# One pinned order for the second chunk's up-projection weights, ahead of the first chunk's convolution

## The chip, the cores and the metric

The kernel runs on one core of a Trainium2 chip. A core has several engines, each with a queue of its own that it works through in order: TensorE (PE, matrix products), VectorE (DVE), ScalarE (ACT), GpSimd (POOL) and SyncE (SP), which here issues nearly all of the DMA transfers. An instruction that depends on another engine waits for a semaphore at the head of its queue, and all that stands behind it waits too. The metric is the time of one execution in device microseconds (us).

## The reference

One layer of a hybrid decoder on 1,024 tokens of width 1,024, after 16 prepended meta tokens. All is in float32.

```python
h = layer_norm(concat(meta, x))
z = h @ w_in + b_in                       # q, k, v, conv input, merge gates
a = sliding_window_attention(q, k, v)     # 8 heads, window 128
c = silu(layer_norm(causal_dwconv(c_val * sigmoid(c_gate), 31 taps)))
mixed = sigmoid(g_attn) * (a @ w_attn_proj) + sigmoid(g_conv) * (c @ w_conv_proj)
h = layer_norm(ALPHA * h + mixed @ w_out)
up = causal_dwconv(h @ ffn_w_up, ffn_dw, ffn_dw_b)      # 3 taps
u, g = split(up, 2)                                     # 2 x 2816 columns
f = (gelu(g) * u) @ ffn_w_down
out = layer_norm(ALPHA * h + f)
```

The change lies in the up projection, `h @ ffn_w_up` with its 3-tap convolution, the gelu and the product `gelu(g) * u`.

## The kernel before

The stages follow each other on TensorE: input projection with the attention and the 31-tap convolution beside it (to about 414 us of the profile), the two branch projections (to 504), the output projection (to 604), the up projection (604 to 1042), the down projection (to 1246) and the last normalization.

**The up projection** makes 22 chunks. Chunk `c` takes 128 gate columns and 128 value columns of `ffn_w_up` (tiles `FC + c` and `c`, 1,024 x 128 each). The product is made by a Strassen-Winograd scheme: the weights' four quadrants `a11`, `a12`, `a21`, `a22` and the activations' four quadrants are first combined into sums, and seven products (`prod`, L1587) take the place of eight. For float32 accuracy each operand is split in a high part (a cast to fp32r on ScalarE) and a low part (raw minus high, on VectorE), and a product is three matrix products high x high, low x high, high x low. The tokens are halved once more in two pieces, `sub` 0 and 1. One of the seven products is 24 matmuls of 256 or 260 columns.

The seven products of a chunk come in the order B11, B21, BT2, BT4, BT1, BT3, B22. They go to four accumulators in PSUM: X (`px`) takes B11, BT2 and BT3 one on top of the other, Z (`pz`) takes B21, V4 (`pw`) BT4, and Y (`py`) BT1 and B22. Between BT2 and BT3 and the like, ScalarE copies what X or Y holds so far (`copy`, L1609). VectorE then puts the four results together (`tt`, L1605): `c11` from Z, later `c22`, `c21` and `c12`.

**Weights.** The generator `up_weights` (L1429) makes a chunk's seven weight operands from two raw tiles `wr` of 512 KB that SyncE loads (`w_rows`, two buffers: the load for the chunk after next waits for the last reader of the tile that it overwrites). In order: `a11` for B11; `a12` for B21; the split of `a22` (for BT4); then three sums on VectorE (L1433): a22 = a21 + a22, a21 = a11 - a21, a11 = a22 - a11; then the split of the new `a11` (BT2), of `a22` (BT1), of `a21` (BT3); a fourth sum, a22 = a12 - a11, and its split (B22). Each split is one cast (`wsplit`, L1414, ScalarE) and one subtraction (L1415, VectorE), 128 x 512 each. The operands lie in a ring of ten places in `RHO` and in tiles `w`; `ring_next` counts them over all chunks, so chunk 0 has 1 to 7 and chunk 1 has 8 to 14. `w_ahead(9)` in `prod` keeps nine operands ahead in the program.

**Convolution.** For each of the four results `conv_ffn` (L1519) takes three small ScalarE steps (L1522 twice, L1524) and two VectorE steps (L1525, L1526); two results go through gelu (L1530), and `f_out` (L1533) multiplies and stores to `fd`, one store a half.

Chunk 0 is made in two passes, `sub` 1 first, because the activations of `sub` 0 come last out of the stage before; the splits of their sums (`split_of`, `bsplit`, L1285) run on VectorE and ScalarE during the first pass. Chunk 1 follows directly. `sums_load` and `sums_form` (L1546, L1552; L1557 to L1560) prepare weights of the down projection: two loads, four sums, two stores a chunk.

**What sets the order.** A list scheduler places the instructions of each engine by its own estimate of when each is ready and by a rank (smaller first; `RK_SUMS` is 470, `RK_CHAIN` for the `tt` and `copy` steps 400, `RK_TURN` 450). `after(x, y)` says only that x stands behind y in the order. `line` strings an instruction behind the one before on a list `lined`; `high` is a like list of ScalarE casts. While `pinned_w` is set, that is for chunk 0's weights, low parts and sums are strung on `lined`. For the first three operands of chunk 1 (`ring_next` to 10) before, a cast was put behind the last of the activation casts and a low part behind a named activation split (`formed`); the rest of chunk 1 was left to the scheduler.

Of the kernel before, what the change touches and what calls it, by code (L numbers as in the profile page):

```python
# [26 lines left out]
OP = mybir.AluOpType  # L27
# [17 lines left out]
FC = DFF // P  # L45
# [14 lines left out]
HW = 514  # L60
# [53 lines left out]
def tile_hybrid_layer(  # L114
# [1291 lines left out]
    def wsplit(src):  # L1406
        i = ring_next[0]
        ring_next[0] += 1
        i %= len(RING)
        if RING[i] is None:  # L1410
            RING[i:i + 2] = wsp_flat()
        t = RING[i]
        hi, lo = t[:, 0:512], t[:, 512:1024]
        cast = nc.scalar.copy(hi, src)  # L1414
        ins = nc.vector.tensor_tensor(lo, src, f32(hi), OP.subtract)  # L1415
        if pinned_w[0]:
            line(ins)
        elif ring_next[0] <= 10:
            after(cast, high[-1])
            after(ins, formed[ring_next[0] - 8])  # L1420
        return hi, lo
# [7 lines left out]
    def up_weights():  # L1429


        def tt(*x):
            ins = nc.vector.tensor_tensor(*x)  # L1433
            if pinned_w[0]:
                line(ins)
# [19 lines left out]

    pinned_w, formed = [True], []
    w_stream = up_weights()
# [60 lines left out]

    def conv_ffn(cc, o):  # L1519
        t = ftmp()  # L1520
# [3 lines left out]
        nc.scalar.activation(t, cc[:, 2:HW], AF.Identity, bias=ffw(3, o), scale=ffw(2, o))  # L1524
        nc.vector.scalar_tensor_tensor(t, cc[:, 1:HW - 1], ffw(1, o), t, OP.mult, OP.add)  # L1525
        nc.vector.scalar_tensor_tensor(t, cc[:, 0:HW - 2], ffw(0, o), t, OP.mult, OP.add)  # L1526
# [49 lines left out]
    for c in range(FC):  # L1576
        Y, V4, Z, X = (pup.tile([P, 1024], F, name=n, tag=n) for n in ("py", "pw", "pz", "px"))
        passes = ((1,), (0,)) if c == 0 else ((0, 1),)
        for subs in passes:
# [7 lines left out]
            def prod(q, bank, first):  # L1587
                if last:
                    w_ahead(9)
                    ah, al = w_ready.pop(0)  # L1590
# [24 lines left out]
            if last and c == 0:  # L1615
                after(high[-2], copied[-1])
            prod(B21, Z, True)
# [5 lines left out]
            if not last:  # L1623
# [5 lines left out]
                form_t3(0, LATE)  # L1629
                for q in (BT2, BT4, BT1, BT3, B22):  # L1630
                    split_of(0, q)
                    formed.append(lined[-1])
                t2_low = formed[0]
                formed[:2] = []
            if last:
                g0 = gelu(conv_ffn(c11, FC + c))
            prod(BT4, V4, True)
# [270 lines left out]
```

## Time and profile before

| what | us |
|---|---|
| median of three runs | 1258.44 (1258.18 to 1258.76) |
| the profiled execution's own time | 1261.86 |
| its span, first to last instruction | 1260.1 |
| 414 to 504 us, branch projections: PE busy | 90.00 of 90.00 |
| 504 to 604 us, output projection: PE busy | 100.00 of 100.00 |
| 1042 to 1246 us, down projection: PE busy | 204.00 of 204.00 |
| 1246 to 1260 us, last normalization: PE busy | 6.00 of 14.00 |

The profile is one execution, recorded by the hardware. In its rows a time is the start from the span's beginning, then the busy time, engine, line, operation, tiles written and read, shape and count; in brackets stands how long the engine was idle before and what ended that. A matmul row of count 12 is one half of one of the seven products.

### The profile page before, as it was taken

Reading aid. Unit: us, or ns where it says so; the run is one execution under the profiler, and the core shown is the slowest. Engines: PE = TensorE matmul, PEld = TensorE weight load, DVE = VectorE, ACT = ScalarE, POOL = GpSimd, SP = SyncE. Lnnn points to the kernel's source line nnn. Section 1 sums busy time; section 2 is a strip of 40 time slices with the busy share of each in tenths; the row PEclk is TensorE's granted clock in tenths of the full one; section 3 lists DMA queues with packets and bytes.
Section 4 is the critical chain, followed back from the end, with each engine's and each line's share of the span. In section 5 each row is a group of like instructions: output and inputs, shape, how many; then the busy total and the mean of one; then the engine's idle time right before and its main releaser. Section 6 shows DMA issues by size and latency. Waiting matters only on the chain.

```text
span 1260.1 us, 23202 instructions
## 1 busy us (share of the span) xinstructions
PE 1242.3 (99%) x9176; PEld 1176.2 (93%) x9176; DVE 1080.4 (86%) x1866; ACT 627.5 (50%) x1280; POOL 7.4 (1%) x8
## 2 busy tenths in 40 slices
PE   8999999999999999999989999999999999999997
PEld 7999999999999999788989999999999998888886
DVE  7988999999978677448989999999899987896697
ACT  7533355655474233344656565665565654445330
POOL 0000000001000000000000000000000000000000
PEclk9999999999999999999999999999999999999999
DMA  6383633332256554222145455553454557999712
GB/s 252 110 300 104 188 98 97 106 97 81 72 159 179 167 155 118 84 100 79 56 151 213 156 207 185 186 209 114 173 210 167 209 204 254 391 354 334 274 61 84
DMA packets 98688, 212.20 MB, mean 168 GB/s; under 512 B 11396, under 2 KB 38596, under 8 KB 98323
## 3 DMA queue, kind: packets, MB, share of 16 engines
q1 hardware_dynamic: 84414, 199.57, 46.5%
q10 hardware_dynamic: 14164, 11.15, 2.8%
q8 instruction: 72, 1.18, 0.4%
q14 instruction: 38, 0.30, 0.1%
HBM read 150.29 MB, written 62.70 MB: 169 GB/s over the span
## 4 chain that ended last, share of the span: by engine, by line
PE 88%; DVE 7%; DMA 3%; ACT 1%; issue 1%; SPq 0%; DVEq 0%; ACTq 0%
PE px L1599 11%; PE ps_x L1754 9%; PE ps_z L340 8%; PE ps_z L343 8%; PE ps_z L344 8%; PE py L1599 8%; PE ps_z L1754 7%; PE ps_p L1172 7%; PE pw L1599 4%; PE pz L1599 4%; PE ps_w L340 2%; PE ps_w L343 2%; PE ps_w L344 2%; PE ps_z L575 2%; PE ps_t L943 1%
## 5 line engine op out<-in xcount | busy, mean ns | idle before, releaser
L340 PE MATMUL ps_z<-RHO,w 128*128 128x256 f32 (+2 forms) x864 | 243.2, 281 | 0.0
L343 PE MATMUL ps_z<-RHO,w 128*128 128x256 f32 (+2 forms) x864 | 242.3, 280 | 0.0
L344 PE MATMUL ps_z<-RHC,w 128*128 128x256 f32 (+2 forms) x864 | 242.2, 280 | 0.0
L343 PEld LDWEIGHTS ps_z<-RHO,w 128*128 128x128 f32 x864 | 162.5, 188 | 0.5
L344 PEld LDWEIGHTS ps_z<-RHC,w 128*128 128x128 f32 x864 | 162.6, 188 | 0.2
L340 PEld LDWEIGHTS ps_z<-RHO,w 128*128 128x128 f32 x864 | 162.5, 188 | 0.1
L749 DVE SCALAR_TENSOR_TENSOR FA<-cin,cdw,FA 128x1026 f32<-128x1026 f32 x120 | 154.3, 1295 | 0.7
L300 ACT CAST w<-wr 128x1024 fp32r<-128x1024 f32 x37 | 38.8, 1048 | 62.6 <-PE ps_z L344 44.5
L1415 DVE TENSOR_TENSOR RHO<-wr,RHO 128x512 fp32r<-128x512 f32 x94 | 64.0, 684 | 2.1 <-ACT RHO L1414 1.7
L1414 ACT CAST RHO<-wr 128x512 fp32r<-128x512 f32 x94 | 57.0, 618 | 17.4 <-DVE wr L1433 10.8
L1433 DVE TENSOR_TENSOR wr<-wr 128x512 f32<-128x512 f32 x88 | 60.1, 683 | 0.2
L758 ACT ACTIVATE FA<-ps_z,colr 128x258 f32<-128x258 f32 (+1 forms) x64 | 30.1, 472 | 59.8 <-PE ps_z L344 46.9
L303 DVE TENSOR_TENSOR w<-wr,w 128x1024 fp32r<-128x1024 f32 x37 | 45.1, 1218 | 7.6 <-ACT w L300 7.4
L1611 ACT COPY FA<-px 128x516 f32<-128x516 f32 (+2 forms) x23 | 13.1, 570 | 72.0 <-PE px L1599 72.0
L1599 PE MATMUL px<-OA,RHO 128*128 128x260 f32 x324 | 44.1, 285 | 4.2 <-ACT RHO L1414 2.4
L1172 PE MATMUL ps_p<-OC,w 128*128 128x256 f32 (+1 forms) x384 | 48.1, 278 | 0.0
L1172 PE MATMUL ps_p<-OA,w 128*128 128x256 f32 (+1 forms) x384 | 47.8, 278 | 0.0
L1172 PEld LDWEIGHTS ps_p<-OC,w 128*128 128x128 f32 x384 | 46.1, 188 | 0.1
L1172 PEld LDWEIGHTS ps_p<-OA,w 128*128 128x128 f32 x384 | 45.9, 188 | 0.0
L1599 PEld LDWEIGHTS px<-OA,RHO 128*128 128x128 f32 x324 | 40.9, 190 | 5.0 <-ACT RHO L1414 2.6
L1415 DVE TENSOR_TENSOR w<-wr,w 128x512 fp32r<-128x512 f32 x60 | 40.8, 685 | 5.2 <-ACT w L1414 5.0
L1414 ACT CAST w<-wr 128x512 fp32r<-128x512 f32 x60 | 36.3, 617 | 13.6 <-DMA wr<-in_w_up_dram 7.4
(457 smaller groups left out, 3117.7 us busy)
## 6 DMA issues: line engine op xcount, KB each, us to landing
wr<-in_w_up_dram SPq DMA_DIRECT2D x44, 512.0 KB, 4.3
wr<-in_w_z_dram SPq DMA_DIRECT2D x29, 512.0 KB, 4.1
OB<-in_w_down_dram SPq DMA_DIRECT2D x24, 512.0 KB, 5.4
fd<-FA SPq DMA_DIRECT2D x44, 256.0 KB, 2.0
FA<-sd SPq DMA_DIRECT2D x15, 512.0 KB, 8.7
qt<-qd SPq DMA_DIRECT2D x28, 256.0 KB, 4.3
OB<-td SPq DMA_DIRECT2D x14, 512.0 KB, 8.7
sgd<-FA ACTq DMA_DIRECT2D x48, 128.0 KB, 2.6
```

What stands on the lines that cost most here:

```text
L300: ins = nc.scalar.copy(hi, raw)
L303: return nc.vector.tensor_tensor(lo, raw, f32(hi), OP.subtract)
L340: ins = nc.tensor.matmul(ps, al, bh, start=i == 0, stop=False)
L343: nc.tensor.matmul(ps, ah, bh, start=False, stop=False)
L344: last = nc.tensor.matmul(ps, ah, bl, start=False, stop=i == n - 1)
L749: nc.vector.scalar_tensor_tensor(acc[c], cin[:, j:j + U], wc, acc[c], OP.mult, OP.add)
L1172: nc.tensor.matmul(ps[:, :b - a], x, rhs(k, hl, a, b), start=k + j == 0, stop=k == 3 and j == 2)
L1414: cast = nc.scalar.copy(hi, src)
L1415: ins = nc.vector.tensor_tensor(lo, src, f32(hi), OP.subtract)
L1433: ins = nc.vector.tensor_tensor(*x)
L1599: ins = nc.tensor.matmul(o, (ah, ah, al)[j][:, k * P:(k + 1) * P], bmat(sub, q, j, k), start=first and i == 0, stop=i == 11, skip_group_ch ...
L1754: nc.tensor.matmul(banks[i], l[:, ts], r[:, ws], start=first and a and x + k == 0, stop=z and x == len(ops) - 1 and k == 2, skip_group_che ...
```

## The change

In words: (1) For operands 8 to 13 of the ring, which are chunk 1's without the last, the casts on ScalarE are strung on `high` in the order in which they are generated, and the low parts on VectorE on `lined`. (2) The three sums of chunk 1 (`ring_next` at 10) are strung on `lined` too; so VectorE has activation splits, low parts of the first three operands, the three sums, the low part of the new `a11`, and then the next low parts in one fixed order. (3) The operands that are generated ahead of products B11 and B21 of chunk 0 get rank `RK_SUMS`. (4) In chunk 0 the first VectorE step of each of the four convolutions (L1525) stands behind the last of `lined` at that point, which is the low part for BT2 of chunk 1. (5) Chunk 1's copy of B11 on ScalarE stands behind the cast for BT2 (`high[7]`), and in chunk 0 the copy after B11 now stands ahead of the fourth activation cast and not ahead of the third. The list `formed` is gone. No instruction is added or removed, none changes its size; the line numbers of the new kernel behind L1417 are up to five higher (L1611 is L1614, L1607 is L1610, L1526 is L1528, L1534 is L1536, L1557 to L1560 are L1559 to L1562).

```diff
-        if pinned_w[0]:
+        if not pinned_w[0] and ring_next[0] <= 13:
+            after(cast, high[-1])
+            high.append(cast)
+        if pinned_w[0] or ring_next[0] <= 13:
             line(ins)
-        elif ring_next[0] <= 10:
-            after(cast, high[-1])
-            after(ins, formed[ring_next[0] - 8])
         return hi, lo
@@ up_weights
         def tt(*x):
             ins = nc.vector.tensor_tensor(*x)
-            if pinned_w[0]:
+            if pinned_w[0] or ring_next[0] <= 10:
                 line(ins)
...
-    def conv_ffn(cc, o):
+    def conv_ffn(cc, o, behind=None):
...
-        nc.vector.scalar_tensor_tensor(t, cc[:, 1:HW - 1], ffw(1, o), t, OP.mult, OP.add)
+        ins = nc.vector.scalar_tensor_tensor(t, cc[:, 1:HW - 1], ffw(1, o), t, OP.mult, OP.add)
+        if behind:
+            after(ins, behind)
         nc.vector.scalar_tensor_tensor(t, cc[:, 0:HW - 2], ffw(0, o), t, OP.mult, OP.add)
@@ prod
                 if last:
-                    w_ahead(9)
+                    with rank(RK_SUMS if c == 0 and q in (B11, B21) else tc.cur_priority):
+                        w_ahead(9)
...
             copy(u13[:, a:b], at(X))
             if last and c == 0:
-                after(high[-2], copied[-1])
+                after(high[3], copied[-1])
+            if c == 1:
+                after(copied[-1], high[7])
...
-                for q in (BT2, BT4, BT1, BT3, B22):
+                split_of(0, BT2)
+                t2_low = lined[-1]
+                for q in (BT4, BT1, BT3, B22):
                     split_of(0, q)
-                    formed.append(lined[-1])
-                t2_low = formed[0]
-                formed[:2] = []
             if last:
-                g0 = gelu(conv_ffn(c11, FC + c))
+                behind = None if c else lined[-1]
+                g0 = gelu(conv_ffn(c11, FC + c, behind))
...
-                f1 = conv_ffn(c22, c)
-                f_out(c, 0, g0, conv_ffn(c21, c))
-                f_out(c, 1, gelu(conv_ffn(c12, FC + c)), f1)
+                f1 = conv_ffn(c22, c, behind)
+                f_out(c, 0, g0, conv_ffn(c21, c, behind))
+                f_out(c, 1, gelu(conv_ffn(c12, FC + c, behind)), f1)
```

How it moves the instructions is seen at three places. The first is VectorE's order around chunk 1's weights. `wr_7241` and `wr_7242` are chunk 1's two raw tiles (`a11`, `a12` and `a21`, `a22`); `pz_7461` is chunk 1's accumulator Z; `FA` and `OB` hold results and convolutions. Before, from the second of the three sums on:

```order
L1433 TENSOR_TENSOR wr_7242<-wr_7241,wr_7242 128x512
L1525 SCALAR_TENSOR_TENSOR FA_78<-OB_81,coll_130,FA_78 128x512
L1525 SCALAR_TENSOR_TENSOR FA_78<-FA_78,coll_130 128x512
L1433 TENSOR_TENSOR wr_7241<-wr_7242,wr_7241 128x512
L1415 TENSOR_TENSOR RHO_80<-wr_7242,RHO_80 128x512
L1526 SCALAR_TENSOR_TENSOR FA_78<-OB_81,coll_130,FA_78 128x512
L1526 SCALAR_TENSOR_TENSOR FA_78<-FA_78,coll_130 128x512
L1525 SCALAR_TENSOR_TENSOR FA_78<-OB_81,coll_130,FA_78 128x512
L1607 TENSOR_TENSOR FA_78<-pz_7461,OB_81 128x516
L1433 TENSOR_TENSOR wr_7242<-wr_7241 128x512
L1415 TENSOR_TENSOR RHO_80<-wr_7242,RHO_80 128x512
L1415 TENSOR_TENSOR RHO_80<-wr_7241,RHO_80 128x512
```

And the change, from the first of the three sums on:

```order
L1433 TENSOR_TENSOR wr_7242<-wr_7242 128x512
L1433 TENSOR_TENSOR wr_7242<-wr_7241,wr_7242 128x512
L1433 TENSOR_TENSOR wr_7241<-wr_7242,wr_7241 128x512
L1415 TENSOR_TENSOR RHO_80<-wr_7241,RHO_80 128x512
L1525 SCALAR_TENSOR_TENSOR FA_78<-FA_78,coll_130 128x512
L1525 SCALAR_TENSOR_TENSOR FA_78<-OB_81,coll_130,FA_78 128x512
L1525 SCALAR_TENSOR_TENSOR FA_78<-FA_78,coll_130 128x512
L1525 SCALAR_TENSOR_TENSOR FA_78<-OB_81,coll_130,FA_78 128x512
L1415 TENSOR_TENSOR RHO_80<-wr_7242,RHO_80 128x512
L1528 SCALAR_TENSOR_TENSOR FA_78<-FA_78,coll_130 128x512
L1415 TENSOR_TENSOR RHO_80<-wr_7242,RHO_80 128x512
L1528 SCALAR_TENSOR_TENSOR FA_78<-OB_81,coll_130,FA_78 128x512
```

The low part of the new `a11` (it reads `wr_7241`) moves from behind three convolution steps, Z's step, the fourth sum and another low part to directly behind its own sum; the convolution of chunk 0 moves behind it. After these rows the change has two more convolution steps, the fourth sum of chunk 1 (it frees tile `wr_7241`), Z's step with `pz_7461`, the two products of `f_out`, and chunk 1's last low part.

The second place is VectorE's order around chunk 2's weights, from raw tiles `wr_7405` (`a11`, `a12`) and `wr_7406` (`a21`, `a22`). Before, from its third low part on, the first two standing just ahead:

```order
L1415 TENSOR_TENSOR w_7238<-wr_7406,w_7238 128x512
L1433 TENSOR_TENSOR wr_7406<-wr_7406 128x512
L1433 TENSOR_TENSOR wr_7406<-wr_7405,wr_7406 128x512
L1415 TENSOR_TENSOR RHO_80<-wr_7406,RHO_80 128x512
L1433 TENSOR_TENSOR wr_7405<-wr_7406,wr_7405 128x512
L1415 TENSOR_TENSOR RHO_80<-wr_7406,RHO_80 128x512
L1433 TENSOR_TENSOR wr_7406<-wr_7405 128x512
L1415 TENSOR_TENSOR w_7238<-wr_7405,w_7238 128x512
L1415 TENSOR_TENSOR RHO_80<-wr_7406,RHO_80 128x512
L1607 TENSOR_TENSOR OB_81<-OB_81 128x516
L1607 TENSOR_TENSOR FA_78<-OB_81,pw_7460 128x516
L1557 TENSOR_TENSOR OB_81<-OB_81 128x512
```

And the change, where `pz_7697` is chunk 2's accumulator Z:

```order
L1610 TENSOR_TENSOR FA_78<-pz_7697,OB_81 128x516
L1528 SCALAR_TENSOR_TENSOR FA_78<-OB_81,coll_130,FA_78 128x512
L1562 TENSOR_TENSOR OB_81<-OB_81 128x512
L1433 TENSOR_TENSOR wr_7406<-wr_7405,wr_7406 128x512
L1415 TENSOR_TENSOR RHO_80<-wr_7406,RHO_80 128x512
L1525 SCALAR_TENSOR_TENSOR FA_78<-FA_78,coll_130 128x512
L1536 TENSOR_TENSOR FA_78<-FA_78 128x512
L1433 TENSOR_TENSOR wr_7405<-wr_7406,wr_7405 128x512
L1415 TENSOR_TENSOR RHO_80<-wr_7406,RHO_80 128x512
L1528 SCALAR_TENSOR_TENSOR FA_78<-FA_78,coll_130 128x512
L1433 TENSOR_TENSOR wr_7406<-wr_7405 128x512
L1415 TENSOR_TENSOR w_7238<-wr_7405,w_7238 128x512
```

Before, all of chunk 2's sums and low parts stood in one piece ahead of chunk 1's results, and the step that reads `pz_7697` came twelve rows after the last row shown. Now they are spread among chunk 1's results and convolutions. Between the first two low parts (which stand behind chunk 1's last) and the rows shown there are, in order: four steps on chunk 1's results and on the down-projection sums (three L1610 and one L1559), three convolution steps, L1560, the third low part, two convolution steps, L1561, the first sum of chunk 2 and one product of `f_out`. The second and third sum of chunk 2 and the low part for its BT2, the last row, stand behind the step that reads chunk 2's own Z.

The third place is ScalarE's order around chunk 3's casts (raw tiles `wr_7611`, `wr_7612`) and the copies of chunk 2's accumulators `px_7698` and `py_7695`. Before:

```order
L1611 COPY FA_78<-px_7698 128x516
L1522 ACTIVATE FA_78<-FA_78 128x1 x2
L1524 ACTIVATE FA_78<-FA_78,coll_130 128x512
L1414 CAST w_7169<-wr_7612 128x512
L1530 ACTIVATE FA_78<-FA_78 128x512
L1414 CAST w_7238<-wr_7612 128x512
L1611 COPY OB_81<-py_7695 128x516
```

And the change:

```order
L1414 CAST RHO_80<-wr_7611 128x512 x2
L1414 CAST RHO_80<-wr_7612 128x512
L1614 COPY FA_78<-px_7698 128x516
L1414 CAST w_7169<-wr_7612 128x512
L1414 CAST w_7238<-wr_7612 128x512
L1414 CAST w_7169<-wr_7611 128x512
L1414 CAST w_7238<-wr_7612 128x512
L1614 COPY OB_81<-py_7695 128x516
```

All seven casts of chunk 3 now stand ahead of the copy of `py_7695`, on top of which chunk 2's B22 is accumulated; before, only five of them did.

On ScalarE the cast for BT2 of chunk 1 stands, in the change, directly behind the last L1524 of chunk 0 and ahead of the copy of chunk 1's X; the table load for gelu and the first gelus stand behind chunk 1's second copy of X. In SyncE's queue the loads `wr_7405`, `fd` store, `wr_7406`, `fd` store, two `OB` loads become `wr_7405`, two `fd` stores, `OB` load, `wr_7406`, `OB` load; and the two loads of chunk 3's raw tiles, which before stood next, now stand behind two stores to `td`, two to `fd` and the two loads of `sums`.

More of the change, by code (lines that the diff above doesn't have):

```diff
@@ L1454, in up_weights @@
             yield p3
-    pinned_w, formed = [True], []
+    pinned_w = [True]
     w_stream = up_weights()
```

## The prediction

> **What bounds the kernel now.** I read the page first, then the stages, then TensorE's waits.
>
> ```profile
> span 1260.1 us, 23202 instructions
> PE 88%; DVE 7%; DMA 3%; ACT 1%; issue 1%; SPq 0%; DVEq 0%; ACTq 0%
> 604.00:651.00 47.00, 42.98 (x344) 41.82 (x343) 42.53 (x77) 28.76 (x59) 0.00 (x0) 0.96 0.28 95
> 651.00:1042.00 391.00, 390.53 (x3363) 390.06 (x3362) 359.25 (x569) 234.26 (x499) 0.00 (x0) 1.00 0.51 187
> ```
>
> The second line is the chain of waits; the last two are stretches: length, then busy time of PE, its weight loads, DVE, ACT and POOL, then the granted clock. PE sets the end. From 651 on it lacks 0.5 us of 391, so nothing is to be won there; from 604 to 651, in chunks 0 and 1, it lacks 4.0 of 47, at a mean clock of 0.96. DVE is 92% busy in the later chunks (359.25 of 391), so what is put off there is caught up slowly. PE's waits from 600 to 700, and PE in order of time:
>
> ```profile
> PE px L1599 <- ACT RHO L1414: 2.4, 1, 2.4
> PE px L1599 <- DVE RHO L1415: 1.4, 1, 1.4
> 625.45 1.59 PE L1599 MATMUL px<-RHC,w 128*128 128x260 f32 x12
> 628.23 1.59 PE L1599 MATMUL pz<-RHO 128*128 128x260 f32 x12
> 629.66 1.52 PE L1599 MATMUL pz<-OC,RHO 128*128 128x256 f32 x12
> 633.58 0.76 PE L1599 MATMUL px<-OA,RHO 128*128 128x260 f32 x4 [2.40 <-ACT RHO L1414]
> 635.70 1.78 PE L1599 MATMUL px<-OA,RHO 128*128 128x260 f32 x8 [1.36 <-DVE RHO L1415]
> 637.28 2.58 PE L1599 MATMUL px<-OC,RHO 128*128 128x256 f32 x12
> 639.70 1.59 PE L1599 MATMUL pw<-OA,RHO 128*128 128x260 f32 x12
> 648.48 1.70 PE L1599 MATMUL py<-RX,RHO 128*128 128x260 f32 x12 [0.26 <-ACT OB L1611]
> 656.98 1.70 PE L1599 MATMUL px<-OA,w 128*128 128x260 f32 x12
> ```
>
> Chunk 1 begins at 625.45, and one product lasts 2.78 (625.45 to 628.23; half of it 1.43). Its third, BT2, waits 2.40 us for the cast of the new `a11`, does four matmuls, and waits 1.36 for the low part. Then matmuls run slow: twelve take 2.42 (637.28 to 639.70). The clock tells why:
>
> ```profile
> 632.68:636.10 3.42, 1.16 (x7) 0.94 (x8) 3.42 (x6) 2.54 (x6) 0.00 (x0) 1.00 0.00 0
> 636.10:639.51 3.41, 3.41 (x18) 3.41 (x18) 3.34 (x6) 0.63 (x1) 0.00 (x0) 0.50 0.81 228
> ```
>
> In a stretch of 3.4 us in which PE was busy for 1.16, the clock stayed; for the next 3.41 it was 0.50, which costs half of that, 1.7. The last PE row is chunk 2's BT2. Nine products at 2.785 behind 625.45 it would begin at 650.5; it begins at 656.98. So all that goes wrong in chunk 1 has cost 6.5 us by then: 2.40 + 1.36 + 0.26 + 1.7, and 0.8 of small steps.
>
> Why is the cast late? ScalarE and VectorE in order of time:
>
> ```profile
> 626.22 0.48 ACT L1522 ACTIVATE OB<-OB 128x1 f32<-128x1 f32 x2 [1.62 <-DVE OB L1607]
> 627.31 0.47 ACT L1522 ACTIVATE FA<-FA 128x1 f32<-128x1 f32 x2
> 630.58 1.28 ACT L1530 ACT_TABLE_LOAD   x1
> 632.41 1.12 ACT L1414 CAST RHO<-wr 128x512 fp32r<-128x512 f32 x2
> 625.10 0.74 DVE L1525 SCALAR_TENSOR_TENSOR FA<-FA,coll 128x512 f32<-128x512 f32 x1
> 625.77 0.42 DVE L1607 TENSOR_TENSOR OB<-OB 128x260 f32<-128x260 f32 x1
> 626.10 0.41 DVE L1607 TENSOR_TENSOR FA<-OB,pw 128x260 f32<-128x260 f32 x1
> 628.64 0.74 DVE L1525 SCALAR_TENSOR_TENSOR FA<-OB,coll,FA 128x512 f32<-128x512 f32 x1
> 629.30 0.74 DVE L1525 SCALAR_TENSOR_TENSOR FA<-FA,coll 128x512 f32<-128x512 f32 x1
> 629.97 0.68 DVE L1433 TENSOR_TENSOR wr<-wr 128x512 f32<-128x512 f32 x1
> 630.57 0.68 DVE L1415 TENSOR_TENSOR RHO<-wr,RHO 128x512 fp32r<-128x512 f32 x1
> 634.36 1.28 DVE L1415 TENSOR_TENSOR RHO<-wr,RHO 128x512 fp32r<-128x512 f32 x2
> 644.61 1.42 DVE L1433 TENSOR_TENSOR wr<-wr 128x512 f32<-128x512 f32 x2
> ```
>
> The third sum (629.97) stands behind convolution steps; the cast then stands behind the table load and a gelu, and the low part, second of the two at 634.36, behind more convolution.
>
> **The change part by part.** No instruction is added, so everything is order. From start to start, a VectorE subtraction of 512 takes 0.60 (629.97 to 630.57), a convolution step 0.66 (628.64 to 629.30), a 260-wide result 0.33 (625.77 to 626.10), a sum that needs the one before 0.71 (half of 1.42); ScalarE's three steps of one convolution take 1.09 (626.22 to 627.31), a cast 0.6.
>
> *Chunk 1, gain.* VectorE is free at 625.10. Three results (1.0) and three sums (2.1): 628.2. ScalarE starts the last three convolutions once the first result stands, at 625.5, and is through at 625.5 + 3 x 1.09 = 628.8; cast to 629.4, low part to 630.1. PE comes to BT2 at 629.66 + 1.36 = 631.0. Both stalls and the half clock go, with 0.9 us to spare. The later operands are in time too: VectorE's rows, four L1525 (2.65), low part for BT1 at 633.3 (PE is there at 636.6), for BT3 at 634.6 (639.4), fourth sum at 637.2, B22's low part at 639.6 (642.1). Chunk 2 could begin at 644.95 in place of 651.4.
>
> *Chunk 2, loss.* Its first raw tile comes free with the fourth sum, at 637.2, which is 1.6 later than before:
>
> ```profile
> 635.67 5.49 DMA wr<-in_w_up_dram
> 641.84 1.29 DVE L1415 TENSOR_TENSOR w<-wr,w 128x512 fp32r<-128x512 f32 x2 [2.40 <-ACT w L1414]
> 649.10 0.58 ACT L1611 COPY OB<-px 128x516 f32<-128x516 f32 x1
> wr<-in_w_up_dram SPq DMA_DIRECT2D x10, 512.0 KB, 3.5
> OB<-in_w_down_dram SPq DMA_DIRECT2D x4, 512.0 KB, 5.1
> sums<-in_w_down_dram SPq DMA_DIRECT2D x2, 512.0 KB, 5.1
> ```
>
> The load took 5.49 there (rows of the chain, of DVE, of a copy on ACT, and of the transfers from 600 to 700 with their median); the median of ten is 3.5. At 5.49 it lands at 642.7 and, as 641.84 follows on 641.16, the low parts start at 643.4 and end at 644.6: in time for B11 and B21. But now VectorE's queue has chunk 1's results and convolutions first. From 644.6: four subtractions (2.4) 647.0; three convolution steps (2.0) 649.0; L1560 and the third low part 650.2; two steps 651.5; L1561, the first sum and a product 653.3; then L1610, which reads chunk 2's own Z (complete at 650.5, so no wait) 653.9; a step 654.6; L1562, second sum, low part 656.4; a step and a product 657.7; third sum 658.3. The cast for BT2 follows at 659.0; the low part, three instructions later, ends at 660.8. PE wants BT2 at 650.5. It waits 8.5 us for the high part, and another 1.3 for the low part (660.8 less 659.0, less 0.48 for four matmuls): 9.8. With the load at 3.5 VectorE comes to L1560 2.0 earlier, at 7.8 in all, but that step needs the second `OB` load, the last of six transfers at 5.1 each or so. I take 9.8, since 5.49 is the row of this very load.
>
> There is a floor that no load moves: L1610 cannot start before PE has finished B21, at 650.5. Eight instructions to the third sum's end (six of 0.60, two of 0.66), 4.9, then the cast, 0.7: BT2 at 656.1, a wait of 5.6, and 1.3 for the low part: 6.9.
>
> *Clock.* A stall that long leaves at least one stretch of 3.4 us without PE work, so half clock returns. Bounds are nothing, if that stretch lies in the wait, and two stretches, 3.4; I take the one case that the rows show, 1.7.
>
> The Trainium skill, "TensorE: Matmul & The Clock Gate", section "HAM oscillation — how this bites in real kernels", warns of gaps in PE's work of over about 3.4 us; it speaks against this change, which gives up two short gaps for one long one. This trace is harsher than that, since gaps of 2.40 and 1.36 already brought 0.50. The same page, section "What's actually happening", has a window of 3413 ns that runs free of the program (the 3.41 us above agree), so work taken up again may meet 0.9 to 2.5 us of loss in place of 1.7, an estimate from that page, by which the sum below would be +4.2 to +5.8.
>
> *Chunk 2's B22 and chunk 3.* Y's copy, without which B22 may not start, stands behind all casts of chunk 3. Chunk 3's tiles come free at 660.2 and 661.5, behind the two `sums` loads; at 5.1 to 5.3 the second lands at 666.7. From there cast 0.65, low part 0.6, two chained sums 1.4, three subtractions 1.8, the fourth sum 0.7, cast 0.65, copy 0.58: 673.1. PE wants B22 at 660.8 + 2.3 (rest of BT2) + 1.7 + 3 x 2.785 = 673.2. So nothing is lost, and nothing is to spare: I take 0, with 0 to 2.4 as bounds (half a load's 5 us). Cast, loads and copies of later chunks stand as before and had 0.5 us of idle in 391.
>
> *Sum.* New loss 9.8 + 1.7 + 0 = 11.5; old loss 6.5. Net **+5.0 us**. On the span that is 1260.1 to 1265.1, on the profiled execution's own 1261.86 to 1266.9. The three runs lie at 1258.44, 3.4 below that execution; the stall is in either, so I forecast **1263.4**.
>
> **The rivals.** Changes within 0.2%, 2.5 us, count as no change.
>
> *Cascade, slower.* If chunk 3's second tile lands 2 us late or more, Y's copy holds B22, and that wait brings a second stretch of half clock, with DVE too full to catch up: 2.4 + 1.7 more, +9.1, 1267.5. For it: no spare in the working above, two stores and two loads ahead in SyncE's queue. Against: tiles landed in 3.5 at the median.
>
> *Near the floor, no change.* Loads at 3.5 and the half clock mostly inside the wait: 6.9 + 0.5 less 6.5, about +1, 1259.3. Against: VectorE's own queue, which is full without any load until 653.9.
>
> *Not slower.* The whole gain comes, 1252.0 (6.5 off): it needs the third sum of chunk 2 to be done before PE's 650.5. The deciding point is L1610 with `pz_7697`: only if VectorE could pass it before B21 ends. For it: chunk 1's two stalls do go. Against: it reads that accumulator, and the floor of 6.9 alone is more than the 6.5.
>
> *The change doesn't do what it says.* ScalarE reaches the cast of chunk 1 over 0.9 us late, behind the convolution's three starts, and BT2 stalls there as well: half clock and some 2 us in chunk 1 stay, chunk 2 is as late as forecast: about +8, 1266.5. Against: 625.5 follows from rows that the change does not move.
>
> **How the numbers follow.** Forecast 0.72; cascade 0.13; near the floor 0.07; not slower 0.04; not what it says 0.04. The forecast's own range is from 6.9 + 1.7 - 6.5 = +2.1 (1260.5) to 9.8 + 2.5 - 6.5 with 1 us of B22, +6.8 (1265.2); the cascade, taken half in, brings the upper end to 1267.0. Range 1260.5 to 1267.0. Slower: 0.72, 0.13 and 0.04, and a little of the floor: 0.90. No change 0.06, faster 0.04.
>
> **What would show it.** In the new profile: no idle before BT2 of chunk 1 near 631 and a clock of 1.00 there; DVE's third sum of chunk 2 (L1433) after the L1610 that reads `pz`; PE idle for 6 to 9 us before `px<-OA,w` near 650 to 659, released by ScalarE's L1414, then about 1.3 released by L1415; 0.50 for 3.4 us behind it; B22 of chunk 2 nearly without wait; the rest of the up projection as before, all later by 5. Wrong if that idle time is under 4 us, if the stall near 631 stays, or if PE waits again and again after 680.

## The result, and the profile after

| | median, us | runs | range, us |
|---|---|---|---|
| before, beside the change | 1258.18 | 7 | 1257.55 to 1259.01 |
| the change | 1262.90 | 7 | 1261.61 to 1264.46 |

The ratio is 1.0038, 95% interval 1.0026 to 1.0049: the change costs 4.7 us, between 3.3 and 6.2. The profiled execution took 1262.64 us.

From the page of the change come the span and the chain; from its windows three stretches (length; busy time of PE, its weight loads, DVE, ACT and POOL; granted clock; share and rate of DMA).

```profile
span 1260.8 us, 23202 instructions
PE 89%; DVE 7%; DMA 1%; ACT 1%; issue 1%; SPq 0%; DVEq 0%; ACTq 0%
604.00:651.00 47.00, 43.57 (x372) 43.06 (x370) 44.41 (x78) 31.11 (x64) 0.00 (x0) 1.00 0.30 107
651.00:700.00 49.00, 44.29 (x357) 43.99 (x358) 41.70 (x67) 26.15 (x54) 0.00 (x0) 0.90 0.47 177
700.00:1043.00 343.00, 342.77 (x2956) 342.58 (x2955) 314.57 (x497) 205.02 (x437) 0.00 (x0) 1.00 0.51 187
```

As before, everything that goes wrong in the up projection goes wrong early: behind 700 us PE lacks 0.2 of 343. But the place has moved. PE's waits from 600 to 700 us, and its rows:

```profile
PE px L1602 <- ACT w L1414: 7.6, 1, 7.6
PE px L1602 <- DVE w L1415: 0.6, 1, 0.6
622.36 1.59 PE L1602 MATMUL px<-RHC,w 128*128 128x260 f32 x12
627.93 1.59 PE L1602 MATMUL px<-OA,RHO 128*128 128x260 f32 x12
641.84 1.59 PE L1602 MATMUL px<-RHC,w 128*128 128x260 f32 x12
646.05 1.52 PE L1602 MATMUL pz<-OC,w 128*128 128x256 f32 x12
655.13 1.24 PE L1602 MATMUL px<-OA,w 128*128 128x260 f32 x4 [7.56 <-ACT w L1414]
656.95 2.09 PE L1602 MATMUL px<-OA,w 128*128 128x260 f32 x8 [0.58 <-DVE w L1415]
658.83 2.73 PE L1602 MATMUL px<-OC,w 128*128 128x256 f32 x12
```

Chunk 1 runs from 622.36 to 641.84, 19.48 us for seven products, with no wait before its BT2 at 627.93. Chunk 2's BT2 then waits 7.56 us for the high part and 0.58 for the low part, and its last twenty matmuls take 4.44 us (656.95 to 661.39, where the next product begins).

VectorE's rows tell why: the fourth sum of chunk 1 and the first low parts of chunk 2 at the top, a down-projection sum that waits for its load, then chunk 2's first sum, the step that reads Z, its second and third sum, and the low part for BT2. Below them ScalarE's casts and SyncE's two issues of raw tiles.

```profile
633.64 0.69 DVE L1433 TENSOR_TENSOR wr<-wr 128x512 f32<-128x512 f32 x1
638.85 1.29 DVE L1415 TENSOR_TENSOR w<-wr,w 128x512 fp32r<-128x512 f32 x2 [0.66 <-ACT w L1414]
641.87 0.69 DVE L1559 TENSOR_TENSOR OB<-OB 128x512 f32<-128x512 f32 x1 [0.52 <-DMA OB<-in_w_down_dram]
648.20 0.68 DVE L1433 TENSOR_TENSOR wr<-wr 128x512 f32<-128x512 f32 x1
649.40 0.69 DVE L1610 TENSOR_TENSOR FA<-pz,OB 128x516 f32<-128x516 f32 x1
651.27 0.68 DVE L1433 TENSOR_TENSOR wr<-wr 128x512 f32<-128x512 f32 x1
653.74 0.68 DVE L1433 TENSOR_TENSOR wr<-wr 128x512 f32<-128x512 f32 x1
656.21 0.68 DVE L1415 TENSOR_TENSOR w<-wr,w 128x512 fp32r<-128x512 f32 x1
```

```profile
638.20 1.14 ACT L1414 CAST w<-wr 128x512 fp32r<-128x512 f32 x2 [1.09 <-DMA wr<-in_w_up_dram]
643.58 0.62 ACT L1414 CAST w<-wr 128x512 fp32r<-128x512 f32 x1 [0.52 <-DMA wr<-in_w_up_dram]
654.46 0.62 ACT L1414 CAST w<-wr 128x512 fp32r<-128x512 f32 x1 [1.85 <-DVE wr L1433]
```

```profile
634.39 0.33 SPq L125 DMA_DIRECT2D wr<-in_w_up_dram  x1
637.45 0.34 SPq L125 DMA_DIRECT2D wr<-in_w_up_dram  x1
```

The tiles lie ready for their casts at 638.20 and 643.58, but the third sum starts at 653.74, and no bracket stands on the last five VectorE rows: the engine was not idle ahead of them. It was doing other work, chunk 1's results, convolution and down-projection sums.

To compare kernels, one number carries best: the time from chunk 1's first product (`px<-RHC,w`) to chunk 3's fourth (`pw<-OA`). It holds 17 products, 47.3 us at 2.785 each, the stalls of chunks 1 to 3 and the half clock, and leaves out the start of the program. Before it is 53.98 (625.45 to 679.43), in the change 58.53 (622.36 to 680.89): +4.55.

### The profile page after: what moved, and what is told of

Read it like the earlier page. It is cut to its first block, busy times and chain, and to the rows that moved or that the text cites. A ratio compares the mean times of both kernels' runs of the same rounds, so it can differ in the third digit from the quotient of the medians.

```text
span 1260.8 us, 23202 instructions
## 1 busy us (share of the span) xinstructions
PE 1241.1 (98%) x9176; PEld 1176.1 (93%) x9176; DVE 1081.0 (86%) x1866; ACT 626.8 (50%) x1280; POOL 7.4 (1%) x8
## 4 chain that ended last, share of the span: by engine, by line
PE 89%; DVE 7%; DMA 1%; ACT 1%; issue 1%; SPq 0%; DVEq 0%; ACTq 0%
PE px L1602 12%; PE ps_x L1759 9%; PE py L1602 8%; PE ps_z L340 8%; PE ps_z L343 8%; PE ps_z L344 8%; PE ps_z L1759 7%; PE ps_p L1172 7%; PE pw L1602 4%; PE pz L1602 4%; PE ps_w L344 2%; PE ps_w L343 2%; PE ps_w L340 2%; PE ps_z L575 2%; PE ps_t L943 1%
## 5 line engine op out<-in xcount | busy, mean ns | idle before, releaser
L1614 ACT COPY FA<-px 128x516 f32<-128x516 f32 (+2 forms) x23 | 13.1, 570 | 74.0 <-PE px L1602 74.0
L1602 PE MATMUL px<-OC,RHO 128*128 128x256 f32 x324 | 41.2, 276 | 0.0
```

The costliest lines, as they stand in the source:

```text
L1602: ins = nc.tensor.matmul(o, (ah, ah, al)[j][:, k * P:(k + 1) * P], bmat(sub, q, j, k), start=first and i == 0, stop=i == 11, skip_group_ch ...
```

## The experiments

Each ran beside the kernel before, in three groups; a ratio is to the runs of the kernel before in its own group, with its 95% interval. "Segment" is the time just defined, in the profiled execution. Diffs are against the change unless said otherwise.

| | segment | waits before chunk 2's BT2 | median | before in its group | ratio |
|---|---|---|---|---|---|
| before | 53.98 | none | | | 1 |
| the change | 58.53 | 7.56 + 0.58 | 1262.90 | 1258.18 | 1.0038 (1.0026 to 1.0049) |
| 1 bounds at 11 | 48.10 | none | 1253.06 | 1259.65 | 0.9949 (0.9937 to 0.9962) |
| 2 the same, sum late | 59.95 | 6.56 + 1.19 | 1264.04 | 1259.65 | 1.0038 (1.0024 to 1.0051) |
| 3 sum first | 55.48 | 0 + 3.60 | 1260.08 | 1259.81 | 1.0005 (0.9996 to 1.0013) |
| 4 raw load first | 57.41 | 2.77 + 3.54 | 1262.44 | 1259.81 | 1.0029 (1.0018 to 1.0039) |
| 5 Z step behind | 57.51 | 7.08 + 0 | 1261.49 | 1259.21 | 1.0019 (1.0010 to 1.0027) |
| 6 convolution not held | 52.75 | 0 + 0.85 | 1258.52 | 1259.21 | 0.9990 (0.9980 to 0.9999) |
| 7 no copy tie | 59.99 | 8.93 + 0.59 | 1263.82 | 1259.81 | 1.0033 (1.0021 to 1.0045) |
| 8 chunk 2 pinned too | 62.15 | 0 + 0.80 | 1270.71 | 1259.21 | 1.0091 (1.0075 to 1.0106) |
| 9 before, filled | 53.75 | 0.60 | 1260.97 | 1259.65 | 1.0009 (1.0000 to 1.0019) |
| 10 change, 50 fillers | 59.59 | 2.71 + 0.58 | 1264.14 | 1259.65 | 1.0034 (1.0022 to 1.0047) |
| 11 change, 55 fillers | 58.33 | 1.76 + 1.06 | 1264.60 | 1259.21 | 1.0044 (1.0032 to 1.0056) |
| 12 change, 68 fillers | 57.03 | 0.24 + 1.06 | 1261.66 | 1259.81 | 1.0019 (1.0010 to 1.0027) |

### What puts chunk 2's sums so late

**1. Fewer operands pinned.**

```diff
-        if not pinned_w[0] and ring_next[0] <= 13:
+        if not pinned_w[0] and ring_next[0] <= 11:
...
-        if pinned_w[0] or ring_next[0] <= 13:
+        if pinned_w[0] or ring_next[0] <= 11:
```

> Both bounds of 13 become 11, so that of chunk 1 only the first four casts and low parts and the three sums are in the pinned order; the low parts for BT1 and BT3, the fourth sum and the last low part are left to the scheduler, which now puts BT1's, BT3's and the fourth sum ahead of the convolution. Theory (the loss of the change arises because the fourth sum, and with it the raw tile of chunk 2, comes free behind chunk 0's convolution, so that chunk 2's sums stand deep in VectorE's queue): the tile is free about 5 us earlier, chunk 2's third sum stands ahead of the Z step, no stall of more than 1 us in chunk 1 or in chunk 2, clock 1.00 in both: 6.5 us of old loss gone and at most 1 us left, 1252 to 1253.5. Rival A (it is the moved convolution itself, which fills VectorE in chunk 1 whatever the sums do): chunk 2 still stalls 6 to 8 us, 1260 to 1263. Rival B (the queue of SyncE and long loads set it): the tile lands late all the same, 1258 to 1262.

It came as the theory had it: 6.6 us faster than the kernel before (0.51%), the best kernel of this study. Its profile, VectorE (fourth sum of chunk 1, third sum of chunk 2, Z step), SyncE, PE, and a stretch:

```profile
627.81 0.68 DVE L1433 TENSOR_TENSOR wr<-wr 128x512 f32<-128x512 f32 x1
643.27 0.68 DVE L1433 TENSOR_TENSOR wr<-wr 128x512 f32<-128x512 f32 x1
650.80 0.69 DVE L1610 TENSOR_TENSOR FA<-pz,OB 128x516 f32<-128x516 f32 x1
629.12 3.58 SPq L125 DMA_DIRECT2D wr<-in_w_up_dram  x2
648.26 1.59 PE L1602 MATMUL px<-OA,w 128*128 128x260 f32 x12
651.00:700.00 49.00, 49.00 (x425) 49.00 (x425) 47.03 (x76) 30.30 (x64) 0.00 (x0) 1.00 0.62 219
```

The fourth sum stands at 627.81 and not at 633.64, its tile is loaded from 629.12 and not from 634.39, and the third sum of chunk 2 starts 7.5 us ahead of the Z step (643.27 against 650.80). BT2 (648.26) follows B21 without a wait.

**2. The same, with that one sum held back.** Against kernel 1:

```diff
+            if ring_next[0] == 12:
+                fourth.append(ins)
...
-        nc.vector.scalar_tensor_tensor(t, cc[:, 0:HW - 2], ffw(0, o), t, OP.mult, OP.add)
+        conv_last[:] = [nc.vector.scalar_tensor_tensor(t, cc[:, 0:HW - 2], ffw(0, o), t, OP.mult, OP.add)]
...
+                if c == 0:
+                    after(fourth[0], conv_last[0])
```

> The kernel with the bounds at 11, and one more tie: the fourth sum of chunk 1 stands behind the last step of chunk 0's convolution, as the scheduler has it in the change. Theory (the place of that one sum decides): the tile comes free near 637 again, the stall before BT2 of chunk 2 is back with 6 to 9 us, half clock too; 1261 to 1264. Rival A (the moved convolution) and rival C (it is the low parts of BT1 and BT3, pinned behind BT2's, that make the difference): as with the bounds at 11 alone, since nothing of these two is altered, 1252 to 1254 by C.

PE's waits from 600 to 700 us show the stall of the change back, and one before chunk 3 with it:

```profile
PE px L1606 <- ACT w L1414: 6.6, 1, 6.6
PE px L1606 <- ACT OB L1618: 1.3, 1, 1.3
PE px L1606 <- DVE w L1415: 1.2, 1, 1.2
```

On VectorE the fourth sum of chunk 1 is late again, and chunk 2's third sum stands behind the Z step again:

```profile
634.10 0.68 DVE L1433 TENSOR_TENSOR wr<-wr 128x512 f32<-128x512 f32 x1
650.39 0.69 DVE L1614 TENSOR_TENSOR FA<-pz,OB 128x516 f32<-128x516 f32 x1
653.52 0.68 DVE L1433 TENSOR_TENSOR wr<-wr 128x512 f32<-128x512 f32 x1
```

One tie on one instruction of 0.60 us moves the ratio from 0.9949 to 1.0038, which is the change's. So the place of the fourth sum, with all that the scheduler moves on account of it, is enough to bring the whole loss; rivals A and C fall.

**3. The change, with that sum ahead of the convolution.** The bounds stay at 13.

```diff
         if behind:
             after(ins, behind)
+            conv.append(ins)
...
+                if c == 0:
+                    for x in conv:
+                        after(x, fourth[0])
```

> The change, with chunk 0's convolution held behind the fourth sum of chunk 1 too, so that the sum stands two low parts behind BT2's and the raw tile comes free some 4 us earlier; the bounds stay at 13. Theory: the tile's early release lets the scheduler put chunk 2's three sums ahead of the Z step, and the stall falls from 8.1 to 0 to 4 us; 1254 to 1259 where the kernel before has 1258.2. If the low bound of 11 and not the place of the sum made the good kernel: 1262 to 1264.

VectorE's rows show the fourth sum of chunk 1, the third sum of chunk 2, the Z step and the low part for BT2:

```profile
629.94 0.69 DVE L1433 TENSOR_TENSOR wr<-wr 128x512 f32<-128x512 f32 x1
647.34 0.68 DVE L1433 TENSOR_TENSOR wr<-wr 128x512 f32<-128x512 f32 x1
651.13 0.69 DVE L1613 TENSOR_TENSOR FA<-pz,OB 128x516 f32<-128x516 f32 x1
652.34 0.68 DVE L1415 TENSOR_TENSOR w<-wr,w 128x512 fp32r<-128x512 f32 x1
```

The high part is in time, since the third sum stands ahead of the Z step. But seven steps stand between that sum and the low part, and PE waits 3.60 us for it. A half clock of 3.41 us follows, and waits of 0.58 and 1.26 us in chunks 2 and 3. Of the change's 4.7 us some 0.3 (by the medians) to 0.6 (by the ratio) are left. With the bounds at 13 the sum's place thus gives back nearly all of the loss, and not the 6.6 us gain of kernel 1.

**4. Is it the load?**

```diff
-            load(raw, w_up[m].rearrange("p k c -> p (k c)"))
+            wload.append(load(raw, w_up[m].rearrange("p k c -> p (k c)")))
...
-            after(load(t[h], (w_dn_v if i < FH else fd)[j + h * FH]),
-                  loads[-1] if loads else f_stores[-1])
+            ins = load(t[h], (w_dn_v if i < FH else fd)[j + h * FH])
+            after(ins, loads[-1] if loads else f_stores[-1])
+            if i == 0:
+                after(ins, wload[5])
```

> The change, with chunk 2's second raw tile issued by SyncE ahead of the first down-projection load instead of behind it. Rival B (the late load of that tile, 6.1 us long, sets the stall): the tile lands 2 to 3 us earlier and the stall falls by as much, 1259 to 1260.5 where the kernel before has 1258.2. Theory (VectorE's queue sets it, and it has work all the while): the sum of the waits before BT2 of chunk 2 stays at 6.5 to 8.5 us, 1261.5 to 1263.

Neither side is quite right. The second tile's cast came at 641.59 in place of 643.58, 2.0 us earlier, and the waits fell by 1.8, from 8.14 to 6.31, a little below what the theory allowed. By start times BT2's fifth matmul, the first to need the low part, came 2.3 us sooner (32.3 us behind chunk 1's start in place of 34.6); the waits alone show less, since the four matmuls between them ran at half clock in the change and at full clock here. VectorE's order had moved too (first sum at 643.46 and not 648.20), so not all of this need be the load's. The ratio, 1.0029, can't be told from the change's. The late second tile goes with about a quarter of the 9.0 us by which that matmul is late in the change; the rest of the stall stays when it lands earlier.

**5. Is it the floor, the Z step that must wait for PE?**

```diff
-            tt(c11[:, a:b], at(Z), u13[:, a:b], OP.add)
+            z = tt(c11[:, a:b], at(Z), u13[:, a:b], OP.add)
+            if c == 2:
+                after(z, lows[17])
```

> The change, with chunk 2's Z step (the L1610 that reads Z) put behind chunk 2's low part for BT2, so that no instruction ahead of the second and third sums waits for TensorE. Floor rival (the Z step sets when the sums can come): the stall falls by about 5 us to 2 or 3, 1257 to 1258.5. Theory (VectorE's queue of chunk 1's results, convolution and down-projection sums sets it; the Z step is one instruction of 0.60 us): the stall before BT2 falls by 0.6 to 1.5 us, 1261.5 to 1262.8 where the kernel before has 1258.2.

The waits fell by 1.06 us (8.14 to 7.08), inside the theory's 0.6 to 1.5, not by 5. In the change itself the Z step starts at 649.40, 1.8 us after PE had finished Z (646.05 + 1.52), so it waited for nothing there. The floor does not set the stall in this kernel.

**6, 7. Two parts of the change alone undone.** The hold of the convolution:

```diff
-                behind = None if c else lined[-1]
+                behind = None
```

> The change without its fourth part: chunk 0's convolution is no longer held behind the low part for BT2 of chunk 1; the pinned lists stay. If the convolution's hold is what takes chunk 1's stalls away: about 1.9 and 1.0 us of wait before BT2 of chunk 1 come back, 0.50 behind them, a stall of 1.5 to 3 us stays before BT2 of chunk 2, and the time is near the kernel before, 1257.5 to 1260. If the pinned lists alone do it: no stall near 631, and the change's 1262.9.

Waits of 1.51 us (now for ScalarE's copy of X, which part 5 puts behind the cast) and 0.65 us and a half clock of 3.41 us are back in chunk 1, and the time is near that before. In chunk 2 only 0.85 us is left, where 1.5 to 3 was expected. With the pinned lists as they are, the hold is what buys chunk 1 and what costs chunk 2. The tie of the copy on ScalarE:

```diff
-            if c == 1:
-                after(copied[-1], high[7])
```

> The change without its fifth part: chunk 1's copy of B11 on ScalarE no longer stands behind the cast for BT2. Theory: this part has no bearing on either gain or loss; the same stall before BT2 of chunk 2, ratio to before 1.003 to 1.0045. If the tie helps the cast come in time: a wait of 0.5 to 1 us comes back before BT2 of chunk 1.

The ratio is the change's within the interval and chunk 1 has no wait: this part has no bearing that these runs can tell.

**8. The same pinning for chunk 2.**

```diff
-        if not pinned_w[0] and ring_next[0] <= 13:
+        lows.append(ins)
+        if not pinned_w[0] and ring_next[0] <= 20:
...
-        if pinned_w[0] or ring_next[0] <= 13:
+        if pinned_w[0] or ring_next[0] <= 20:
...
-            if pinned_w[0] or ring_next[0] <= 10:
+            if pinned_w[0] or ring_next[0] in (10, 17):
...
-                behind = None if c else lined[-1]
-                g0 = gelu(conv_ffn(c11, FC + c, behind))
+                behind = lows[10 + 7 * c] if c < 2 else None
+                g0 = gelu(conv_ffn(c11, FC + c, None if c else behind))
...
-                sums_form(c - 1 if c <= FH else c - 2, ins)
+                sums_form(c - 1 if c <= FH else c - 2, lows[17] if c == 1 else ins)
```

> The change carried on to chunk 2: its casts, low parts and first three sums are strung on the same lists, and chunk 1's convolution and the down projection's sums stand behind chunk 2's low part for BT2. VectorE has the same work. Theory (VectorE is full here, so what an order puts off must be done before the next chunk's sums): the stall before BT2 of chunk 2 falls to 0.5 to 1.5 us, and one of 7 to 10 us stands before BT2 of chunk 3; 1262 to 1268. Rival (the order of chunk 2 alone was at fault): no long stall in either, 1252 to 1255.

```profile
651.02 1.23 PE L1603 MATMUL px<-OA,w 128*128 128x260 f32 x8 [0.80 <-DVE w L1415]
679.58 1.23 PE L1603 MATMUL px<-OA,w 128*128 128x260 f32 x4 [9.09 <-ACT w L1414]
682.06 2.09 PE L1603 MATMUL px<-OA,w 128*128 128x260 f32 x8 [1.25 <-DVE w L1415]
```

The stall leaves chunk 2 (0.80) and comes back larger in chunk 3 (9.09 + 1.25, where the change had 8.14). At 1270.71 the kernel is slower than the 1262 to 1268 expected, with 13.65 us of half clock in the up projection. Nothing is won by giving a chunk precedence over the work of the chunk before: VectorE, which in the change is busy 44.41 of the 47 us from 604 on, has to do that work before it comes to the next chunk's sums.

### What the half clock costs

All four kernels put extra matrix products into the gap before BT2 and leave the rest as it is. Those of 9 and 10 have `start=True, stop=True`, and the output of these two isn't the reference's, otherwise than their expectations say; the amount of work is the same. Those of 11 and 12 have `start=False, stop=False`, as in the lines below, which are kernel 12's, and leave X as it should be.

```diff
+                        if c == 2 and q == BT2 and sub == 0 and i in (0, 4):
+                            for _ in range(68 if i == 0 else 0):
+                                gap.append(nc.tensor.matmul(X[:, 768:1024], spare[0][:, 0:P], bmat(1, B21, 0, 0),
+                                                            start=False, stop=False, skip_group_check=True))
```

**9. The kernel before, its two gaps filled** (18 and 5 products, `c == 1`).

> The kernel before, with 18 such extra products in the first gap before BT2 of chunk 1 (2.1 of 2.40 us) and 5 in the second (0.6 of 1.36 us); order of VectorE and ScalarE as before; output unchanged. Theory: the old loss of 6.5 holds 1.7 us of half clock, which goes; some of it comes back as waits for Y's copy and for chunk 2's raw tile, which were met 0.3 us late at half clock: 1256.5 to 1257.5 against 1258.2. Rival (the two gaps are too short to bring the half clock in most runs, the one in the profile was chance): 1258.0 to 1258.4.

The clock held at 1.00 through the up projection, and the time did not fall: ratio 1.0009, at best the same, so the theory's gain of 0.7 to 1.7 us did not come. The rival's figure is nearer. Its reason, that the half clock of the one profile was chance, is not settled, since one execution of the kernel before was profiled. The rows give another reason. Chunk 1's fourth product begins 12.6 us behind its first, in place of 14.3, so 1.6 us is gained there; then new waits take it, for ScalarE's copies of Y and X:

```profile
646.70 1.69 PE L1609 MATMUL py<-RX,RHO 128*128 128x260 f32 x12 [1.01 <-ACT OB L1623]
655.92 1.70 PE L1609 MATMUL px<-OA,w 128*128 128x260 f32 x12 [0.60 <-ACT OB L1623]
```

Chunk 3's fourth product begins 53.75 us behind chunk 1's first, in place of 53.98. In the profile before, the half clock in chunk 1 was thus hidden: PE came late to operands and copies that would have been late without it.

**10, 11. The change, gap filled in part** (50 and 55 products).

> The change, with 50 extra matrix products (128 x 256, into columns of X that nobody reads) between B21 and BT2 of chunk 2, about 6.0 us of the 7.6 us in which TensorE stood still; the order of VectorE and ScalarE there is that of the change. The output does not change. This prices the half clock alone. Theory: the stall stays, the clock holds at 1.00, the last 20 matmuls of BT2 take 2.3 in place of 4.4 us: 1260.4 to 1261.2, that is 1.7 to 2.5 below the change's 1262.9. Rival (the clock costs nothing, since what follows has slack or waits anyway): 1262.5 to 1263. If the fillers delay BT2, over 1263.5.

> The change, with 55 extra matrix products (128 x 256, 6.4 us) between B21 and BT2 of chunk 2, added onto columns of X that nobody reads and without starting a sum there; VectorE's, ScalarE's and SyncE's order is that of the change throughout. With 50 of them a gap of 2.7 us was left and the clock fell to 0.50 all the same, for 6.8 us; here 1 to 2 us should be left. If the half clock of the change costs its 2 us: clock 1.00 there, and 2 us less than the change, ratio to before 1.002. Rival (what follows BT2 waits for chunk 3's loads anyway, as filling the gaps of the kernel before brought nothing): ratio 1.0030 to 1.0045, as the change, with new waits of about 2 us before B22 of chunk 2 or BT2 of chunk 3.

Neither settled it. The gap varied (8.5 and 8.2 us here, fillers included, against 7.7 in the change, all reckoned from two full products behind chunk 2's start), what was left was enough for the clock to fall, for 6.83 and 3.41 us, and the ratios are the change's within their intervals.

**12. Gap filled nearly whole.**

> As with 55 extra products, but 68 of them (7.9 us), which fill the gap before BT2 of chunk 2 nearly whole; VectorE's order is the change's up to chunk 3, where some rows trade places. If the half clock costs the change its 2 us on the path: clock 1.00 there, the last 20 matmuls of BT2 in 2.3 us, 2 us less than the change, ratio to before 1.002. Rival (what follows has a limit of its own): ratio 1.003 to 1.0045, with new waits of 1 to 2 us in chunk 2's B22 or chunk 3.

```profile
656.39 0.75 PE L1612 MATMUL px<-OA,w 128*128 128x260 f32 x4 [0.24 <-ACT w L1414]
658.21 1.22 PE L1612 MATMUL px<-OA,w 128*128 128x260 f32 x8 [1.06 <-DVE w L1415]
```

The clock held, the ratio fell to 1.0019, and PE waits nowhere else up to 720 us. The fall by 0.0019 of 1258 us is 2.4 us, but the two intervals, from different groups, just overlap, so the time alone does not settle it. The rows give 2.0, as the last twenty matmuls took 4.44 us in the change and take 2.47 here (658.21 to 660.68, where the next product begins). The segment fell by 1.5, since BT2 began 0.4 us later here (33.2 us behind chunk 1's start in place of 32.8). In the change the half clock lies on the path: the rows behind it come earlier when it goes.

## Why the prediction was right

Forecast: slower by 5.0 us, 1263.4. Measured: slower by 4.7 (3.3 to 6.2), 1262.9. Point by point:

- **Chunk 1's gain came.** Both waits and the half clock there are gone. BT2's low part was foreseen 4.65 us behind chunk 1's start (630.1 less 625.45); it ended 4.9 behind it, and BT2 began 0.7 later, where 0.9 to spare had been reckoned. The old loss is the segment before, 53.98, less the 47.35 of 17 products without a wait: 6.6, where the prediction had 6.5. Kernel 1, which has no stall in chunk 2, comes within 0.75 of the 47.35.
- **The mechanism of the loss is the one named**: VectorE's queue, with chunk 1's results, convolutions and down-projection sums ahead of chunk 2's second and third sums. No idle time stands on the rows from chunk 2's first sum on, and kernels 2, 3 and 8 move the stall by moving VectorE's order, in 2 and 3 together with the release of the raw tile.
- **Its size was 0.8 us too large.** The 9.8 forecast is how late BT2's fifth matmul is, the first to need the low part. It began 34.6 us behind chunk 1's start (656.95 less 622.36) where nine products and four matmuls make 25.5, so it was 9.0 late. The idle time in the rows is less, 8.14, because the four matmuls between the two waits ran at half clock: 1.24 us, and not the 0.48 reckoned, so the wait for the low part shrank to 0.58. The mis-sized term is the load of the first tile, 5.49 us from the row of before; it took 3.8 (634.39 to 638.20), and VectorE's first low parts of chunk 2 came 1.5 us sooner than foreseen. Of that 0.5 went to a wait that the working did not have, that of L1559 for its load (641.87), and the third sum ended 32.1 us behind chunk 1's start against 32.85 foreseen. The second tile, which the prediction did not tell apart, was issued 3.06 us after the first, behind two stores and one load, and took 6.1 (637.45 to 643.58). Kernel 4 suggests that its lateness had a part in what is left.
- **The half clock was mis-sized the other way**: 1.7 taken, where the last twenty matmuls took 4.44 us, 2.1 more than at full clock (2.785 less 0.48) and 2.0 more than in kernel 12. The prediction's estimate from the Trainium skill, "TensorE: Matmul & The Clock Gate", section "What's actually happening", of 0.9 to 2.5 holds it. The trace has 0.50 for three stretches, 10.24 us, where the prediction had one and at most two. PE worked in 5.69 of them, and the part in BT2's first four matmuls cost nothing: the fifth began 1.82 us behind the first here and in kernel 12 alike, when its low part was there.
- **The two misses partly cancel.** Measured, the sum is 9.0 + 2.1 - 6.6 = 4.5, and the segment grew by 4.55; forecast were 9.8 + 1.7 - 6.5 = 5.0. So the number is a little nearer than its terms.
- **One step was wrong, without harm to the sum.** The old loss was itemized as 2.40 + 1.36 + 0.26 + 1.7 + 0.8, as if each could be had alone. Kernel 9 shows that the 1.7 could not: with the clock back, PE waits for the copies instead. The sum of 6.5 stood because it was taken between two places on PE's line, and not from the items.
- **B22 of chunk 2** was taken at 0 and has no wait.
- **Rivals.** The cascade did not come. The floor (6.9) and its point, the Z step, did not set the stall: kernel 5 moves that step away and gains 1.06 us. The change does what it says in chunk 1. The "not slower" rival needed the third sum ahead of 650.5; kernel 1 reaches that, not by passing the Z step while it waits, as that rival had it, but with the sums in the queue long before it. That the fourth sum's place decides this was not seen in the prediction, which took its lateness of 1.6 us as a matter of the load only.

Three things stay open. Why the list scheduler places chunk 2's sums by the tile's release as it does was not tried apart from the release itself: kernels 1 to 3 move both. Parts 2 and 3 of the change, the pinned sums and the rank, were not undone alone. And the segments move a little otherwise than the medians: in kernel 7 by +6.0 against +4.0, in kernel 3 by +1.5 against +0.3, in kernel 8 by +8.2 against +11.5; one execution and a median over several are not the same, and behind chunk 3 kernel 8 has further waits of 1.1 and 0.7 us.

## What to carry to other kernels

Pinning an order ahead of other work on an engine that is nearly full can borrow its time from the next stage: before pinning, find the instruction that frees the buffer which the next stage loads into, and see on which side of the moved work it falls. Here the same idea with two operands fewer, which leaves that instruction in front, turned +4.7 us into -6.6. And a low clock or a wait in a profile is worth only what the next limit behind it allows: fill it or take it away by itself before counting it as gain.

## What the runs showed of the hardware

- **The clock goes by stretches of 3.41 us, and by how busy PE was in the one before.** With such stretches laid on the records, PE was busy in the one ahead of each fall to 0.50 for 1.55 of 3.41 us at most (kernel 8, at the start of the program); it was 1.16 in the kernel before, 1.09 in kernel 11, 0.76 in kernel 10. One with 1.91 of 3.41 did not bring it (before, at 629.27). In kernel 4 a stretch with 1.53 was still followed by 1.00, so the border lies near there and is not sharp in these traces.
- **Coming back takes a nearly full stretch.** The change and kernel 10, by stretches:

```profile
647.75:651.16 3.41, 0.00 (x0) 0.00 (x0) 3.41 (x6) 1.65 (x4) 0.00 (x0) 1.00 0.24 90
651.16:654.57 3.41, 0.00 (x0) 0.00 (x0) 3.41 (x7) 1.40 (x4) 0.00 (x0) 0.50 0.38 154
654.57:657.99 3.42, 2.28 (x9) 1.98 (x10) 3.01 (x5) 1.72 (x3) 0.00 (x0) 0.50 0.93 283
657.99:661.40 3.41, 3.41 (x18) 3.41 (x18) 0.00 (x0) 0.40 (x1) 0.00 (x0) 0.50 0.96 388
```

```profile
656.40:659.81 3.41, 2.77 (x11) 2.46 (x12) 2.52 (x4) 1.23 (x3) 0.00 (x0) 0.50 0.98 296
659.81:663.23 3.42, 3.42 (x18) 3.42 (x18) 0.18 (x1) 0.83 (x2) 0.00 (x0) 0.50 0.87 353
```

  With 2.28 and 2.77 of 3.41 busy the clock stayed at 0.50 for the next stretch; full ones, and one with 2.91 in kernel 11, ended it. Without the 0.58 us of wait inside BT2 the stretch with 2.28 would have had about 2.86, between the two, so whether that wait cost the third slow stretch is not shown.
- **The start of the program varies by 3 us.** In the profiled execution before, the first normalized rows came late and the clock fell; in that of the change neither happened:

```profile
11.19 0.33 PE L518 MATMUL ps_h<-coll,xn 128*128 128x128 f32 x1 [2.46 <-DVE xn L497]
```

```profile
9.63 0.33 PE L518 MATMUL ps_h<-coll,xn 128*128 128x128 f32 x1 [0.83 <-DVE xn L497]
```

  The up projection began at 604.30 in the one and at 601.38 in the other. Of the fourteen profiles three show 0.50 at the start: before, kernel 6 and kernel 8. If the timed executions mostly start as the change's did, these 2.9 us are most of the 3.4 by which the profiled execution of before lay above the median ahead of the change, and would explain why the profiled times of the two kernels stand only 0.8 us apart.
